# Order dependencies on VectorE in the mixing stage: the inverse's second X before two conv taps and four masked shares, one softmax division before three subtractions of TT

## The chip, the cores and the metric

The kernel runs on one core of one Trainium2 chip. The metric is the device time of one execution in microseconds (us), lower is better. The core has five engines with a queue each: PE (TensorE, matrix products; its weight loads are shown as PEld), DVE (VectorE), ACT (ScalarE), POOL (GpSimd) and SP (SyncE, which issues DMAs here). Each engine takes its instructions strictly in the order in which they were written into its queue, and waits for others by semaphores.

## The reference

Two layers, each a half-step SwiGLU feed-forward, a token mixing and another half-step feed-forward, on 512 tokens of width 1024. Only the mixing is touched. It has three groups of heads side by side:

```python
hn = rms_norm(h, g_mix[l]) * (1.0 + sc2) + sh2
proj = hn @ w_mix_in[l]
p_att, p_rwkv, p_conv = jnp.split(proj, [ATT_PROJ_WIDTH, ATT_PROJ_WIDTH + RWKV_PROJ_WIDTH], axis=-1)
y_att = sliding_window_sink_attention(p_att, ...)   # softmax over a window of 128, blocks of 128 tokens
y_rwkv = rwkv7_time_mix(p_rwkv, ...)                # a linear recurrence over the tokens
y_conv = short_conv_mix(p_conv, conv_w[l])          # u = c_gate * h; three taps over time; b_gate * y
mixed = jnp.concatenate([y_att, y_rwkv, y_conv], axis=-1) @ w_mix_out[l]
h = h + (1.0 + gt2) * mixed
```

## The kernel before, in words

Activations are kept transposed (features on the 128 partitions, 512 tokens along the free dimension). Every large product is made in three passes (`mm3`, L129 to L131), a high and a low part of each operand, and so each block of weights costs a cast to its high part on ACT (L141, `wH`) and a subtraction for its low part on DVE (L143, `wL`), after which its raw buffer is free for the next load from SP (L304).

The mixing (`mix`) weaves four generators into one program: `products()` (the large products `ps_mm`, and the short convolution), `rwkv()`, `attention()` and `inverse()`. A loop with an estimated clock decides whose next step is issued; a scheduler behind it then sets the order on every engine, bounded by data dependencies and by order dependencies written by hand (`tc.add_manual_dep(later, earlier, ORDER)`: the first stands behind the second, and no semaphore is added for it). On PE the small products of the three other generators (all at L787, helper `pe`) stand between the large ones.

The parts that meet around the change, in each layer:

- **The recurrence** is made in chunks of 64 tokens, and needs an inverse of a triangular matrix for each chunk and head, built up in two levels (`invert`, inside `rwkv`). T and TT are the inverse so far and its transpose, each in two tiles (one for each pair of heads). In a level, PE makes `ps_x` (B by T), DVE masks it into X (L1124, six instructions for the two tiles), PE makes `ps_t` from X, and DVE subtracts that from TT, and in the first level from T too (L1135, three instructions for a tile). The second level starts with the other tile first. `ps_x` of the second level goes into the PSUM banks that `ps_t` of the first has left. After the second level PE makes `ps_w` from TT.
- **Attention** goes by four blocks of 128 tokens, with two groups g of heads each. DVE reduces the scores (L1319), ACT makes the exponentials and their sums, DVE adds the sink to the sum (L1356, `den`), inverts it (L1357) and multiplies the 128x512 scores `Sc` by it (L1358: the division, which leaves the shares). PE transposes the shares (`ps_pt`), DVE masks each transpose twice (L1345, `pmc` for the block's own keys, `pmp` for the block before: the masked shares), and PE multiplies them with the values (`ps_av`, four products in the order pmc, pmc, pmp, pmp).
- **The short convolution** makes `conv_u` (L923), its first tap by a scalar (L925), two more taps (L926, L927) and the gate (L929), all on DVE, once for each of two blocks of channels.

In both layers the second level of the inverse falls together with the third block of attention (b == 2) and the first block of channels of the convolution.

Of the kernel before, what the change touches and what calls it, by code (L numbers as in the profile page):

```python
# [12 lines left out]
ALU = mybir.AluOpType  # L13
AXL = mybir.AxisListType
ORDER = mybir.DependencyInfo(mybir.DependencyClass.NoSync, mybir.DependencyReason.DATA)
SYNC = mybir.DependencyInfo(mybir.DependencyClass.Sync, mybir.DependencyReason.DATA)

P = 128
D = 1024
T = 512  # L20
# [6 lines left out]
NB = T // P  # L27
# [43 lines left out]
def trunk_kernel(ctx, tc, ins, out, layers=L, phases=("ffn1", "mix", "ffn2")):  # L71
# [11 lines left out]
    tt, stt, ts = nc.vector.tensor_tensor, nc.vector.scalar_tensor_tensor, nc.vector.tensor_scalar  # L83
# [96 lines left out]
    def cst(name):  # L180
        a, b = CON[name]
        return con[:, a:b]

    def rep(name, n):
        a = cst(name)
        return a.unsqueeze(1).to_broadcast([P, n, a.shape[1]])
# [543 lines left out]
    def mix(l, hn, ss, mp, then, ready):  # L730
# [34 lines left out]
        mu, cwp = prm(l, "mu"), prm(l, "cw")  # L765
        cm = small_.tile([P, KD], F32, name="cm", tag="cg")
        ts(cm, mod[l, 5], 1.0, None, ALU.add)

        done = set()
        k_, r_, v_, yr = {}, {}, {}, {}  # L770
        got = {}

# [50 lines left out]
        def products():  # L823
# [93 lines left out]
            for q in range(2):  # L917
                pt = yield from tile_()
                cc = EA("conv_c")
                nc.scalar.copy(pt.like(cc), pt.view)  # L920
                pt = yield from tile_()
                u = EA("conv_u")
                tt(pt.like(u), pt.view, pt.like(cc), ALU.mult)  # L923
                cv = mp.tile([P, T], F32, name="conv_y", tag="cv", bufs=1) if q == 0 else EA("conv_y")
                ts(cv, u, cwp[:, 4 + q : 5 + q], None, ALU.mult)  # L925
                stt(cv[:, 1:], u[:, : T - 1], cwp[:, 2 + q : 3 + q], cv[:, 1:], ALU.mult, ALU.add)  # L926
                stt(cv[:, 2:], u[:, : T - 2], cwp[:, q : q + 1], cv[:, 2:], ALU.mult, ALU.add)  # L927
                pt = yield from tile_()
                tt(pt.like(cv), pt.view, pt.like(cv), ALU.mult)  # L929
                yc.append(cv)  # L930
# [85 lines left out]
        def rwkv():  # L1016
# [91 lines left out]
            def invert():  # L1108

                T_, TT = got["T"], got["TT"]  # L1110
                X = [S(q, "X", (P, 2, NB, CH)) for q in range(2)]

                def each(q, pts, j, lhs, rhs):
                    for b, e, c in corners:
                        pe(pts[q][e][rows[c ^ e], j, b], lhs[q][rows[c], e, b], rhs[q][rows[c], e, b], start=True, stop=True)

                for lev in range(2):
                    qs = both()
                    pts = quarters("ps_x")
                    for q in qs:  # L1120
                        each(q, pts, 0, LT, T_)
                    for q in qs:
                        for r, e, x in gathered(pts[q], 0):
                            tt(X[q][r, e], x, rep(f"lev{lev}", NB)[r], ALU.mult)  # L1124
                    yield 1.4, 3.2
                    qs = both()
                    pts = quarters("ps_t", 2 - lev)
                    for q in qs:
                        if lev == 0:
                            each(q, pts, 1, TT, X)  # L1130
                        each(q, pts, 0, X, TT)
                    for q in qs:
                        for j, to in ((1, T_), (0, TT))[lev:]:
                            for r, e, x in gathered(pts[q], j):
                                tt(to[q][r, e], to[q][r, e], x, ALU.subtract)  # L1135
                        yield (2.4 - 1.0 * lev if q == qs[0] else 0), 2.8 - 1.2 * lev
            pairs(be, B_, 0, 1)
            LT = [B[:, :, :, 0] for B in B_]
# [9 lines left out]
            qs = both()  # L1148
# [23 lines left out]
            qs = both()  # L1172
# [5 lines left out]
            qs = both()  # L1178
# [9 lines left out]
            qs = both()  # L1188
# [14 lines left out]
            qs = both()  # L1203
# [11 lines left out]
            qs = both()  # L1215
# [15 lines left out]
            qs = both()  # L1231
# [17 lines left out]
            for c in range(1, NC - 1):  # L1249
                qs = both()  # L1250
# [7 lines left out]
            qs = both()  # L1258
# [15 lines left out]
            qs = both()  # L1274
# [13 lines left out]
        def attention():  # L1288

            kt, V, qr, rq = got["kt"], got["V"], got["qr"], got["rq"]  # L1290
            snk = prm(l, "sinks").rearrange("p (i g) -> p g i", g=2)

            def scores(b):
                qs = slice(b * P, (b + 1) * P)
                both = [mp.tile([P, 4, P], F32, name="Sc", tag="Sc", bufs=2) for _ in range(2)]
                if b == 0:
                    for Sc in both:
                        nc.gpsimd.memset(Sc, -1e30)
                for i0 in (0, 2):
                    pts = [psum([P, 2, 2, P], "ps_sc") for _ in range(2)]  # L1300
                    for i in range(2):
                        for g, pt in enumerate(pts):
                            if b:
                                m = pe(pt[:, i].rearrange("p a c -> p (a c)"), qr[rows[g], i0 + i, qs], kt[rows[g], (b - 1) * P : (b + 1) * P], start=True, stop=True)
                            else:
                                m = pe(pt[:, i, 1], qr[rows[g], i0 + i, qs], kt[rows[g], qs], start=True, stop=True)
                            together(m, free[0], SYNC)
                    for Sc, pt in zip(both, pts):
                        if b:
                            nc.scalar.copy(Sc[:, i0 : i0 + 2], pt[:, :, 0])  # L1310
                        free[0] = nc.vector.copy_predicated(Sc[:, i0 : i0 + 2], rep("mq", 2).bitcast(I32), pt[:, :, 1])
                    if i0 == 0:
                        yield 1.06, 1.8
                return both

            def softmax(b, g, Sc):
                rqb = rq.rearrange("p (b i g) -> p b g i", i=4, g=2)[:, b, g]
                mx = small("mx", 4)
                nc.vector.tensor_reduce(mx, Sc, AXL.X, ALU.max)  # L1319
                tt(mx, mx, rqb, ALU.mult)  # L1320
                tt(mx, mx, snk[:, g], ALU.max)
                ts(mx, mx, -1.0, None, ALU.mult)
                es = small("es", 4)
                tt(es, snk[:, g], mx, ALU.add)
                act(es, es, AF.Exp)
                den = small("den", 4)
                for i in range(4):
                    act(Sc[:, i], Sc[:, i], AF.Exp, bias=mx[:, i : i + 1], scale=rqb[:, i : i + 1], accum_out=den[:, i : i + 1])
                return den, es

            made, free = [None], [None]

            def together(m, other, kind=ORDER):

                if other is not None:
                    tc.add_manual_dep(m.ins, other.ins.name, kind, reason="both groups run together")

            def turned(b, Sc):
                pt = psum([P, 4, P], "ps_pt")
                for i in range(4):  # L1340
                    pe(pt[:, i], Sc[:, i], cst("ident"), start=True, stop=True, is_transpose=True)
                both = []
                for name, src in (("mc", b), ("mp", b - 1))[: 1 + (b > 0)]:
                    t = E("p" + name)
                    made[0] = tt(t.rearrange("p (i q) -> p i q", q=P), pt, rep(name, 4), ALU.mult)  # L1345
                    both.append((t, src))
                return both

            for b in range(NB):
                qs = slice(b * P, (b + 1) * P)  # L1350
                pm = []
                both = yield from scores(b)
                dens = [softmax(b, g, Sc) for g, Sc in enumerate(both)]
                for g, (Sc, (den, es)) in enumerate(zip(both, dens)):
                    yield 1.06 * (g == 0), 6.4 if g == 0 else 1.2
                    tt(den, den, es, ALU.add)  # L1356
                    nc.vector.reciprocal(den, den)  # L1357
                    tt(Sc, Sc, den.unsqueeze(2).to_broadcast([P, 4, P]), ALU.mult)  # L1358
                    yield 0, 1.4
                    pm.append(turned(b, Sc))  # L1360
                yield 0.4, 3.0
                po = psum([P, 4, P], "ps_av")
                for n in range(len(pm[0])):
                    for g in range(2):
                        t, src = pm[g][n]
                        m = pe(po[rows[g]].rearrange("p i q -> p (i q)"), V[:, src, rows[g]], t, start=n == 0, stop=n == len(pm[0]) - 1)
                        together(m, made[0])
                free[0] = nc.scalar.copy(qr[:, :, qs], po)
                yield 1.9, 1.0
            done.add("ya")  # L1370
# [29 lines left out]
        for q in range(2):  # L1400
            x = pair("yr")
# [203 lines left out]
    with tc.tile_pool(name="first", bufs=1) as fp:  # L1605
        hn, first, ready, casts = begin(fp)
    for n, (l, p) in enumerate(seq):
# [23 lines left out]
        first = None  # L1631
# [87 lines left out]
```

## Time and profile before

| what | value |
|---|---|
| runs | 1793.84, 1797.02, 1799.68 us; median 1797.02 us |
| the profiled execution's own time | 1795.08 us |
| its span | 1793.3 us (1.8 us of the time lie outside it) |
| PEld | 1613.4 us busy (90%) |
| DVE | 1383.6 us busy (77%) |
| ACT | 856.4 us busy (48%) |
| POOL | 148.3 us busy (8%) |
| mean granted PE clock | 0.999 of full speed |

Busy time says how much of the span an engine spent inside instructions. In the timeline a row is a run of equal instructions: start, length, engine, line, operation, `out<-in`, sizes, count, and in brackets how long the engine had been idle before it and what released it. A list of waits gives, for a waiting engine and tile, who released it: total us, times, longest.

### The profile page before, as it was taken

Reading aid. Unit: us, or ns where it says so; the run is one execution under the profiler, and the core shown is the slowest. Engines: PE = TensorE matmul, PEld = TensorE weight load, DVE = VectorE, ACT = ScalarE, POOL = GpSimd, SP = SyncE. Lnnn points to the kernel's source line nnn. Section 1 sums busy time; section 2 is a strip of 40 time slices with the busy share of each in tenths; the row PEclk is TensorE's granted clock in tenths of the full one; section 3 lists DMA queues with packets and bytes.
Section 4 is the critical chain, followed back from the end, with each engine's and each line's share of the span. In section 5 each row is a group of like instructions: output and inputs, shape, how many; then the busy total and the mean of one; then the engine's idle time right before and its main releaser. Section 6 shows DMA issues by size and latency. Waiting matters only on the chain. (4 is left out here: it accounts for less than half of the span.)

```text
span 1793.3 us, 34028 instructions
## 1 busy us (share of the span) xinstructions
PE 1764.2 (98%) x13952; PEld 1613.4 (90%) x13952; DVE 1383.6 (77%) x2224; ACT 856.4 (48%) x1324; POOL 148.3 (8%) x233
## 2 busy tenths in 40 slices
PE   9999999999999999999999999999999999999998
PEld 7898999987778999899899989999876798999998
DVE  7877678877768877677888777887686788864897
ACT  7452355365444554255355515543644345533563
POOL 0101001000000011100100010010000000010000
PEclk9999999999999999999999999999999999999999
DMA  9667867522133676877737597773320427684764
GB/s 377 222 183 266 225 193 214 184 88 79 51 111 103 178 190 215 266 195 208 238 116 191 170 308 189 205 227 103 119 71 28 142 80 203 183 245 132 202 165 118
DMA packets 95436, 313.08 MB, mean 175 GB/s; under 512 B 10864, under 2 KB 13168, under 8 KB 94256
## 3 DMA queue, kind: packets, MB, share of 16 engines
q1 hardware_dynamic: 65088, 203.68, 33.5%
q0 software_dynamic: 30192, 107.23, 24.2%
q8 instruction: 109, 1.79, 0.4%
q14 instruction: 47, 0.39, 0.1%
HBM read 306.93 MB, written 3.93 MB: 173 GB/s over the span
## 5 line engine op out<-in xcount | busy, mean ns | idle before, releaser
L141 ACT CAST wH<-wraw 128x1024 fp32r<-128x1024 f32 (+2 forms) x276 | 254.2, 928 | 439.9 <-PE ps_mm L130 200.5
L143 DVE TENSOR_TENSOR wL<-wraw,wH 128x1024 fp32r<-128x1024 f32 (+2 forms) x276 | 295.3, 1074 | 111.6 <-ACT wH L141 110.2
L129 PE MATMUL ps_mm<-actH,wH 128*128 128x512 f32 (+1 forms) x700 | 253.9, 363 | 1.5 <-DVE h L343 1.5
L131 PE MATMUL ps_mm<-actH,wL 128*128 128x512 f32 (+1 forms) x700 | 253.4, 362 | 0.1
L130 PE MATMUL ps_mm<-actL,wH 128*128 128x512 f32 (+1 forms) x700 | 253.3, 362 | 0.0
L129 PE MATMUL ps_mm<-hnH,wH 128*128 128x512 f32 (+1 forms) x712 | 248.5, 354 | 3.3 <-ACT hnH L291 3.0
L130 PE MATMUL ps_mm<-hnL,wH 128*128 128x512 f32 (+1 forms) x712 | 246.3, 347 | 0.3
L131 PE MATMUL ps_mm<-hnH,wL 128*128 128x512 f32 (+1 forms) x712 | 245.3, 346 | 0.6 <-DVE wL L143 0.6
L434 PE MATMUL ps_d<-comH,wH 128*128 128x256 f32 x864 | 239.2, 277 | 0.1
L436 PE MATMUL ps_d<-comH,wL 128*128 128x256 f32 x864 | 238.2, 276 | 0.0
L435 PE MATMUL ps_d<-comL,wH 128*128 128x256 f32 x864 | 238.2, 276 | 0.0
L143 DVE TENSOR_TENSOR wL<-sum,wH 128x1024 fp32r<-128x1024 f32 x110 | 134.6, 1225 | 81.3 <-ACT wH L141 81.2
L141 ACT CAST wH<-sum 128x1024 fp32r<-128x1024 f32 x110 | 115.1, 1047 | 122.8 <-PE ps_f L435 39.2
L199 DVE SCALAR_TENSOR_TENSOR wada<-wada,crep 128x1024 f32<-128x1024 f32 x128 | 153.1, 1220 | 26.0 <-DMA wada<-in_wadaT 25.7
L434 PEld LDWEIGHTS ps_d<-comH,wH 128*128 128x128 f32 x864 | 166.2, 192 | 2.0 <-ACT s L460 1.6
L436 PEld LDWEIGHTS ps_d<-comH,wL 128*128 128x128 f32 x864 | 166.3, 192 | 0.0
L435 PEld LDWEIGHTS ps_d<-comL,wH 128*128 128x128 f32 x864 | 166.3, 192 | 0.0
L129 PEld LDWEIGHTS ps_mm<-hnH,wH 128*128 128x128 f32 x712 | 133.9, 190 | 23.6 <-issue 7.6
L129 PEld LDWEIGHTS ps_mm<-actH,wH 128*128 128x128 f32 x700 | 133.1, 190 | 16.8 <-DVE h L343 1.7
L131 PEld LDWEIGHTS ps_mm<-hnH,wL 128*128 128x128 f32 x712 | 135.8, 191 | 13.7 <-DVE wL L143 1.0
L130 PEld LDWEIGHTS ps_mm<-hnL,wH 128*128 128x128 f32 x712 | 135.8, 191 | 13.1 <-DVE hnL L292 1.3
L131 PEld LDWEIGHTS ps_mm<-actH,wL 128*128 128x128 f32 x700 | 133.1, 190 | 15.6 <-DVE wL L143 0.5
(426 smaller groups left out, 4006.0 us busy)
## 6 DMA issues: line engine op xcount, KB each, us to landing
wada<-in_wadaT POOLq DMA_DIRECT2D x126, 512.0 KB, 4.7
wraw<-in_wmi SPq DMA_DIRECT2D x40, 512.0 KB, 3.5
wraw<-in_w2p SPq DMA_DIRECT2D x36, 512.0 KB, 4.2
wraw<-in_w1p SPq DMA_DIRECT2D x32, 512.0 KB, 4.3
wraw<-in_w1o SPq DMA_DIRECT2D x32, 384.0 KB, 4.7
wraw<-in_w2o SPq DMA_DIRECT2D x32, 384.0 KB, 4.1
wraw<-in_w1o SPq DMA_DIRECT2D x32, 320.0 KB, 3.7
sum<-in_w2p SPq DMA_DIRECT2D x18, 512.0 KB, 4.3
```

Of the source, the lines that this page charges most:

```text
L129: mm(acc, wH, xH, start=start, stop=False)
L130: mm(acc, wH, xL, start=False, stop=False)
L131: latest["large"] = mm(acc, wL, xH, start=False, stop=stop)
L141: latest["cast"] = nc.scalar.copy(hi, src)
L143: return nc.vector.tensor_sub(lo, src, hi.bitcast(F32))
L199: stt(w, w, 1.0, crep, ALU.mult, ALU.mult, accum_out=out_)
L434: mm(acc, wH, xH, start=start and i + k == 0, stop=False, skip_group_check=True)
L435: mm(acc, wH, xL, start=False, stop=False, skip_group_check=True)
L436: mm(acc, wL, xH, start=False, stop=k == 3, skip_group_check=True)
```

## The change

Three lists are filled and used for order dependencies; no instruction is added, removed or altered. `held` has the two later taps of the first block of channels and the four masked shares of the third attention block; each must now stand behind the X of the second level. `turns` has the three subtractions of the second TT tile in the first level; each must now stand behind the division of the third block's first group.

```diff
-        done = set()
+        done, held, turns = set(), [], []
...
-                stt(cv[:, 1:], u[:, : T - 1], cwp[:, 2 + q : 3 + q], cv[:, 1:], ALU.mult, ALU.add)
-                stt(cv[:, 2:], u[:, : T - 2], cwp[:, q : q + 1], cv[:, 2:], ALU.mult, ALU.add)
+                held.append(stt(cv[:, 1:], u[:, : T - 1], cwp[:, 2 + q : 3 + q], cv[:, 1:], ALU.mult, ALU.add))
+                held.append(stt(cv[:, 2:], u[:, : T - 2], cwp[:, q : q + 1], cv[:, 2:], ALU.mult, ALU.add))
...
-                            tt(X[q][r, e], x, rep(f"lev{lev}", NB)[r], ALU.mult)
+                            new = tt(X[q][r, e], x, rep(f"lev{lev}", NB)[r], ALU.mult)
+                    for later in held if lev else ():
+                        tc.add_manual_dep(later.ins, new.ins.name, ORDER, reason="the inverse goes first")
...
-                                tt(to[q][r, e], to[q][r, e], x, ALU.subtract)
+                                new = tt(to[q][r, e], to[q][r, e], x, ALU.subtract)
+                                if lev == 0 and j == 0 and q == qs[1]:
+                                    turns.append(new)
...
                     made[0] = tt(t.rearrange("p (i q) -> p i q", q=P), pt, rep(name, 4), ALU.mult)
+                    if b == 2:
+                        held.append(made[0])
...
-                    tt(Sc, Sc, den.unsqueeze(2).to_broadcast([P, 4, P]), ALU.mult)
+                    share = tt(Sc, Sc, den.unsqueeze(2).to_broadcast([P, 4, P]), ALU.mult)
+                    for later in turns if (b, g) == (2, 0) else ():
+                        tc.add_manual_dep(later.ins, share.ins.name, ORDER, reason="shares go first")
```

In the built program the order changes on DVE alone, at these places and in both layers alike. (The changed file has a few lines more, so that its L1137 is L1135 before, L1349 is L1345, and L1362 to L1364 are L1356 to L1358.)

First place, DVE at the end of the inverse's first level, in the first layer: T_4518 and TT_4520 are the second tiles of T and TT. Before:

```order
L1135 TENSOR_TENSOR T_4518<-T_4518,ps_t 128x256
L1135 TENSOR_TENSOR T_4518<-T_4518,ps_t 64x256 x2
L1135 TENSOR_TENSOR TT_4520<-TT_4520,ps_t 128x256
L1135 TENSOR_TENSOR TT_4520<-TT_4520,ps_t 64x256 x2
L1356 TENSOR_TENSOR den<-den,es 128x4 x2
L1357 RECIPROCAL den<-den 128x4 x2
L1358 TENSOR_TENSOR Sc<-Sc,den 128x512 x2
```

and with the change:

```order
L1137 TENSOR_TENSOR T_4518<-T_4518,ps_t 128x256
L1137 TENSOR_TENSOR T_4518<-T_4518,ps_t 64x256 x2
L1362 TENSOR_TENSOR den<-den,es 128x4
L1363 RECIPROCAL den<-den 128x4
L1364 TENSOR_TENSOR Sc<-Sc,den 128x512
L1137 TENSOR_TENSOR TT_4520<-TT_4520,ps_t 128x256
L1137 TENSOR_TENSOR TT_4520<-TT_4520,ps_t 64x256 x2
L1362 TENSOR_TENSOR den<-den,es 128x4
L1363 RECIPROCAL den<-den 128x4
L1364 TENSOR_TENSOR Sc<-Sc,den 128x512
```

The first group's three instructions have moved ahead of the three subtractions, and the two groups, which stood in pairs, now stand apart.

Second place, DVE a little further on, from the low part of a weight block to the gate of the convolution: X_4714 and X_4715 are the two tiles of X. Before:

```order
L143 TENSOR_TENSOR wL<-wraw,wH 128x1024
L926 SCALAR_TENSOR_TENSOR conv_y<-conv_u,par,conv_y 128x511
L1345 TENSOR_TENSOR pmc<-ps_pt,con 128x512
L927 SCALAR_TENSOR_TENSOR conv_y<-conv_u,par,conv_y 128x510
L1345 TENSOR_TENSOR pmp<-ps_pt,con 128x512
L1124 TENSOR_TENSOR X_4715<-ps_x,con 128x256
L1124 TENSOR_TENSOR X_4715<-ps_x,con 64x256 x2
L1124 TENSOR_TENSOR X_4714<-ps_x,con 128x256
L1124 TENSOR_TENSOR X_4714<-ps_x,con 64x256 x2
L1345 TENSOR_TENSOR pmc<-ps_pt,con 128x512
L1345 TENSOR_TENSOR pmp<-ps_pt,con 128x512
L929 TENSOR_TENSOR conv_y<-ps_mm,conv_y 128x512
```

and with the change:

```order
L143 TENSOR_TENSOR wL<-wraw,wH 128x1024
L1124 TENSOR_TENSOR X_4715<-ps_x,con 64x256
L1124 TENSOR_TENSOR X_4715<-ps_x,con 128x256
L1124 TENSOR_TENSOR X_4715<-ps_x,con 64x256
L1124 TENSOR_TENSOR X_4714<-ps_x,con 64x256
L1124 TENSOR_TENSOR X_4714<-ps_x,con 128x256
L1124 TENSOR_TENSOR X_4714<-ps_x,con 64x256
L926 SCALAR_TENSOR_TENSOR conv_y<-conv_u,par,conv_y 128x511
L1349 TENSOR_TENSOR pmc<-ps_pt,con 128x512
L927 SCALAR_TENSOR_TENSOR conv_y<-conv_u,par,conv_y 128x510
L1349 TENSOR_TENSOR pmp<-ps_pt,con 128x512
L1349 TENSOR_TENSOR pmc<-ps_pt,con 128x512
```

The six instructions of X stand directly behind the weight block, and two taps and two masked shares have moved behind them, ahead of the other two masked shares. Behind these rows come, before, the gate (L929), the low part of a 128x768 weight block (L143) and the six subtractions of TT; with the change the gate stands between the subtractions of the two TT tiles, and the weight block behind all six.

Third place, PE, whose order is the same, with the semaphores that its rows wait for, from `ps_t` of the second level to `ps_av` of the third block. Before:

```order
L787 MATMUL ps_t<-TT_4519,X_4714 64x64 [waits DVE_49,PE_49]
L787 MATMUL ps_t<-TT_4519,X_4714 64x64 x15
L787 MATMUL ps_t<-TT_4520,X_4715 64x64 x16
L129 MATMUL ps_mm<-hnH,wH 128x512
L130 MATMUL ps_mm<-hnL,wH 128x512
L131 MATMUL ps_mm<-hnH,wL 128x512
L787 MATMUL ps_av<-pmc,V 64x512
L787 MATMUL ps_av<-pmc,V 64x512 [waits DVE_49]
L787 MATMUL ps_av<-pmp,V 64x512
L787 MATMUL ps_av<-pmp,V 64x512 [waits DVE_49]
```

and with the change:

```order
L787 MATMUL ps_t<-TT_4519,X_4714 64x64 [waits DVE_49,PE_49]
L787 MATMUL ps_t<-TT_4519,X_4714 64x64 x15
L787 MATMUL ps_t<-TT_4520,X_4715 64x64 x16
L129 MATMUL ps_mm<-hnH,wH 128x512
L130 MATMUL ps_mm<-hnL,wH 128x512
L131 MATMUL ps_mm<-hnH,wL 128x512
L787 MATMUL ps_av<-pmc,V 64x512 [waits DVE_49] x2
L787 MATMUL ps_av<-pmp,V 64x512
L787 MATMUL ps_av<-pmp,V 64x512 [waits DVE_49]
```

The first of the four `ps_av` now waits for DVE itself, up to the first group's `pmp`, where an earlier wait of PE had covered it. `ps_t` starts with X_4714, the tile that DVE writes last. In the same way the first and the third product of `ps_x` of the second level now wait for the first and the last subtraction of TT_4520, which free its PSUM banks.

## The prediction

> **What bounds the kernel now.** I read the page's first part, then PE's list of waits, then the timeline of the two places that the change touches.
>
> ```profile
> PE 1764.2 (98%) x13952; PEld 1613.4 (90%) x13952; DVE 1383.6 (77%) x2224; ACT 856.4 (48%) x1324; POOL 148.3 (8%) x233
> ...
> PE ps_t L787 <- DVE X L1124: 4.6, 2, 2.3
> ...
> PE ps_pt L787 <- DVE Sc L1358: 1.7, 2, 0.9
> ```
>
> PE is busy for 98% of the span, so time can be won only where PE stands still, or where its clock is low. Two of its waits belong to the change: `ps_t` for X, 2.3 us in each of the two layers, and `ps_pt` for the division, 0.9 us in each. They add up to 6.3 us. In the first layer they lie here (PE's rows):
>
> ```profile
> 475.85 0.38 PE L131 MATMUL ps_mm<-hnH,wL 128*128 128x512 f32 x1
> 477.09 0.63 PE L787 MATMUL ps_pt<-con,Sc 128*128 128x128 f32 x4 [0.87 <-DVE Sc L1358]
> 477.65 1.16 PE L787 MATMUL ps_x<-T,B 64*64 64x64 f32 x64
> ...
> 484.98 1.16 PE L787 MATMUL ps_t<-TT,X 64*64 64x64 f32 x64 [2.29 <-DVE X L1124]
> ...
> 486.92 1.08 PE L787 MATMUL ps_av<-pmc,V 128*64 128x512 f32 x4
> ...
> 488.78 0.48 PE L129 MATMUL ps_mm<-hnH,wH 128*128 128x512 f32 x1
> ...
> 491.34 1.98 PE L787 MATMUL ps_w<-AX,TT 64*64 64x128 f32 x64
> ```
>
> PE had its work until 476.22 and 482.69, and both times waited for DVE. DVE in the same stretch:
>
> ```profile
> 474.53 1.29 DVE L1135 TENSOR_TENSOR TT<-TT,ps_t 128x256 f32<-128x256 f32 x3
> 475.85 0.24 DVE L1356 TENSOR_TENSOR den<-den,es 128x4 f32<-128x4 f32 x2
> ...
> 476.25 1.29 DVE L1358 TENSOR_TENSOR Sc<-Sc,den 128x512 f32<-128x512 f32 x2
> 477.46 0.68 DVE L923 TENSOR_TENSOR conv_u<-ps_mm,conv_c 128x512 f32<-128x512 f32 x1
> ...
> 478.59 1.22 DVE L143 TENSOR_TENSOR wL<-wraw,wH 128x1024 fp32r<-128x1024 f32 x1
> 479.72 0.74 DVE L926 SCALAR_TENSOR_TENSOR conv_y<-conv_u,par,conv_y 128x511 f32<-128x511 f32 x1
> 480.38 0.68 DVE L1345 TENSOR_TENSOR pmc<-ps_pt,con 128x512 f32<-128x512 f32 x1
> 480.99 0.74 DVE L927 SCALAR_TENSOR_TENSOR conv_y<-conv_u,par,conv_y 128x510 f32<-128x510 f32 x1
> 481.64 0.68 DVE L1345 TENSOR_TENSOR pmp<-ps_pt,con 128x512 f32<-128x512 f32 x1
> 482.24 2.59 DVE L1124 TENSOR_TENSOR X<-ps_x,con 128x256 f32<-128x256 f32 x6
> 484.86 0.69 DVE L1345 TENSOR_TENSOR pmc<-ps_pt,con 128x512 f32<-128x512 f32 x1
> 485.47 0.68 DVE L1345 TENSOR_TENSOR pmp<-ps_pt,con 128x512 f32<-128x512 f32 x1
> 486.07 0.68 DVE L929 TENSOR_TENSOR conv_y<-ps_mm,conv_y 128x512 f32<-128x512 f32 x1
> 486.67 0.95 DVE L143 TENSOR_TENSOR wL<-wraw,wH 128x768 fp32r<-128x768 f32 x1
> 487.53 2.59 DVE L1135 TENSOR_TENSOR TT<-TT,ps_t 128x256 f32<-128x256 f32 x6
> ```
>
> No row has a bracket: DVE does not wait at all from 474.53 to 490.12. It is the bound of this stretch, and PE gets its operands when DVE comes to them. An order can therefore choose which of PE's products is served first; it cannot make DVE's sum smaller. That is the main thing to see here, because all four masked shares are still due before `ps_av`, which stands only 2 us behind `ps_t` on PE.
>
> **The change part by part, first layer.** No duration changes, so I walk DVE and PE through the new order with the distances between starts in the rows above.
>
> The division apart. In pairs, `den`, reciprocal and division of both groups take 477.46 - 475.85 = 1.61. Alone they take, from the fourth block:
>
> ```profile
> 501.13 0.17 DVE L1356 TENSOR_TENSOR den<-den,es 128x4 f32<-128x4 f32 x1 [1.86 <-ACT Sc L1328]
> 501.33 0.18 DVE L1357 RECIPROCAL den<-den 128x4 f32<-128x4 f32 x1
> 501.55 0.69 DVE L1358 TENSOR_TENSOR Sc<-Sc,den 128x512 f32<-128x512 f32 x1
> ```
>
> 0.42 from `den` to the division, since each waits for the one before, and then 0.605 to the next instruction (half of 477.46 - 476.25). Twice 1.03 is 2.05: DVE loses 0.44. The first group's sums are there in time:
>
> ```profile
> 473.20 0.19 ACT L1328 ACTIVATION_READ_ACCUMULATOR Sc<-Sc,mx,rq 128x1 f32 x1
> ```
>
> That is the fourth sum of the group, ended at 473.39; `den` can start at 474.53. The division then runs from 474.95 to 475.64, the three subtractions of TT from 475.56 to 476.85, the second division from 477.30 to 477.99, and `conv_u` starts at 477.90.
>
> `ps_pt` and `ps_x`. From the end of a DVE instruction to PE's start I take 0.15 (X ends at 482.24 + 2.59 = 484.83, `ps_t` starts at 484.98; the division ends at 476.94, `ps_pt` starts at 477.09). The shares are ready at 475.79, before PE needs them at 476.22: the wait of 0.87 is gone. But `ps_x`, 0.56 later, now has a wait that was covered before: its third product needs the bank that the last subtraction of TT frees, at 476.85 + 0.15 = 477.00, where PE would be at 476.81. So 0.19 comes back, and PE is 0.68 ahead.
>
> X and `ps_t`. X stands directly behind the weight block, whose next start is 479.72 + 0.44 = 480.16. Six instructions take 2.62 (482.24 to 484.86) and end at 482.75. PE is there at 482.69 - 0.68 = 482.01 and waits until 482.90. The wait shrinks from 2.29 to 0.89, and PE is 484.98 - 482.90 = 2.08 ahead.
>
> `ps_av`. Behind X now come tap, `pmc`, tap, `pmp` of the first group (0.66, 0.61, 0.65 and 0.60 apart, as in the rows), then `pmc` and `pmp` of the second. They end at 485.38 (first `pmp`), 485.99 and 486.59. PE arrives at 486.92 - 2.08 = 484.84. The first product waits for the first `pmp` until 485.53, which is 0.69; a product takes (488.78 - 486.92) / 4 = 0.465; the second waits for its `pmc` until 486.14; the third and fourth follow, the last `pmp` being ready at 486.74. PE is through at 487.53 where it was at 488.78. **1.25 us are left** of 3.16: three new waits of 0.19, 0.69 and 0.15 and a rest of 0.89 stand where 0.87 and 2.29 were.
>
> What follows. `ps_w` needs TT. The six subtractions, with the gate between them, end at 489.74 and are ready at 489.89; PE comes at 491.34 - 1.25 = 490.09. The slack is 0.2, so the lead passes, just. Behind `ps_w` the rows hang on PE, and nothing there has a time of its own.
>
> The 128x768 weight block ends at 490.70, not 487.62, and that is what lets SP issue the next load:
>
> ```profile
> 487.64 0.33 SPq L304 DMA_DIRECT2D wraw<-in_wmo  x1
> ...
> 506.41 0.83 ACT L141 CAST wH<-wraw 128x768 fp32r<-128x768 f32 x1 [2.10 <-PE ps_mm L130]
> ...
> wraw<-in_wmo SPq DMA_DIRECT2D x16, 384.0 KB, 3.0
> ```
>
> The load would be issued some 3.1 later and land 3.0 later again, near 494; the cast that uses it starts at 506.41 and waits for PE's old weights. I cost this at nothing; it is covered by about 12 us. The gate L929, 1.8 later, feeds a high part cast tens of rows further on: nothing too.
>
> Second layer. The rows are the same to 0.01 until `ps_t`; then the clock differs:
>
> ```profile
> 1370.86 1.16 PE L787 MATMUL ps_t<-TT,X 64*64 64x64 f32 x64 [2.30 <-DVE X L1124]
> ...
> 1371.95 0.68 PE L129 MATMUL ps_mm<-hnH,wH 128*128 128x512 f32 x1
> ...
> 1376.30 0.48 PE L129 MATMUL ps_mm<-hnH,wH 128*128 128x512 f32 x1
> ...
> 1372.00:1374.00 2.00, 2.00 (x8) 0.97 (x7) 1.99 (x5) 0.00 (x0) 0.00 (x0) 0.53 0.04 8
> 1374.00:1376.30 2.30, 2.30 (x8) 0.46 (x4) 1.94 (x5) 0.00 (x0) 0.00 (x0) 0.67 0.55 171
> ```
>
> The granted clock was 0.53 and 0.67 there, and from the first L129 to the next after `ps_av` took 1376.30 - 1371.95 = 4.35, against 488.78 - 486.07 = 2.71 in the first layer. This cold spell costs 1.64. It begins 1.1 behind the wait for X, and I find no other inside the span's body; so I book it to that idle time. With no gap over 0.9 left I take it as gone.
>
> Sum: 2 x 1.25 + 1.64 = **4.1 us**.
>
> [...]
>
> Bounds of what the trace does not show. Best: both waits vanish whole, 3.16 a layer. Worst for the order itself: every `ps_av` behind the last `pmp`, 486.74 + 1.86 = 488.60, still 0.18 ahead in each layer. I take 1.25, because PE's waits are single and go by product.
>
> **Against which time.** The sum is made against the profiled execution, 1795.08 us (span 1793.3): 1790.9. That run lies 1.9 under the median of 1797.02. If the 1.9 is a second spell (1.64, in the first layer), the median would lose 2.5 + 3.3 and come to 1791.2; if it is something else, it loses 4.1 and comes to 1792.9. The mean of the three, 1791.7, is my number.
>
> **The rivals.**
>
> *The waits go whole.* If the masked shares were ready in time (PE's semaphores sit elsewhere than I read them, or DVE overlaps more), 2 x 3.16 + 1.64 = 8.0 us: 1787.1 from the profiled run. For it: the rows of before show no wait of `ps_av`. Against it: DVE has no idle time to give, and the masked shares move 2.6 us later or stay, while PE comes 2 us earlier.
>
> *The spell stays or moves.* The gap of 2.29 in the first layer did nothing, so the spell may hang on something else, such as the small 64x64 products around the wait. Then 2.5 us remain: 1792.6 from the profiled run, 1794.5 from the median.
>
> [...]
>
> That the change does nothing can be ruled out: the built order has moved as it says.
>
> **How the numbers follow.** A measurement of this kernel tells about 0.3% (5.4 us) from no change. Forecast 0.55; since 1791.7 is 5.3 under the median, it falls on either side of that bound alike, and I give it 0.30 faster, 0.25 same. Waits whole 0.15, all faster. Spell stays 0.20, same but for 0.02. Slower mechanism 0.10, of which 0.06 beyond the bound. Together: faster 0.47, same 0.47, slower 0.06. The range 1787 to 1797 holds the forecast, the full gain and the spell that stays, and leaves out most of the slower case.
>
> **What would show it.** Right: no wait of `ps_pt` for the division; a wait of `ps_t` for X near 0.9; new waits of `ps_av` for `pmc` or `pmp` near 0.7; `ps_w` without a wait for TT; no granted clock under 0.97 in the second layer's stretch. Wrong: `ps_av` starting without a wait (the full gain), a wait at `ps_w`, or low clocks in both layers.

## The result, and the profile after

| | before | after |
|---|---|---|
| median | 1799.68 us (11 runs, 1793.84 to 1802.61) | 1793.96 us (11 runs, 1791.88 to 1798.8) |
| ratio after to before | | 0.9978, 95% interval 0.9968 to 0.9989 |
| profiled execution, its span | 1795.08, 1793.3 us | 1794.78, 1793.0 us |

The kernel is faster by 0.22% (0.11% to 0.32%), some 3.9 us. The ratio isn't that of the two medians, which differ by 5.7 us (the means of the runs by 4.7); the text goes by the ratio and its interval. The prediction had 1791.7 us, which lies 5.3 us under the median it started from; its own sum was 4.1. It took 0.3% for the least that a measurement tells from no change, and so gave "same" as much chance as "faster"; with eleven runs on each side the interval is some 0.1% to either side, and a ratio of 1 lies outside it. The two profiled executions differ by 0.3 us only, so the gain isn't read from their spans. It is read from the stretch that the change touches, and from the clocks of all runs.

PE's list of waits, after (three rows of it: who waits, for whom, total us, times, longest):

```profile
PE ps_t L787 <- DVE X L1124: 2.2, 2, 1.1
PE ps_o L787 <- issue: 2.0, 2, 1.1
...
PE ps_av L787 <- DVE pmp L1349: 1.1, 2, 0.5
```

`ps_pt` is gone from the list, the wait for X has halved, and a wait of `ps_av` for a masked share is new. The wait of `ps_o`, of which the prediction had said nothing, had been longer before:

```profile
PE ps_o L787 <- issue: 2.7, 2, 1.5
```

PE's timeline after, first layer, from the last large product ahead of `ps_pt` to the first behind `ps_av`:

```profile
478.21 0.38 PE L131 MATMUL ps_mm<-hnH,wL 128*128 128x512 f32 x1
478.43 0.60 PE L787 MATMUL ps_pt<-con,Sc 128*128 128x128 f32 x4
478.96 1.48 PE L787 MATMUL ps_x<-T,B 64*64 64x64 f32 x64
...
485.41 1.16 PE L787 MATMUL ps_t<-TT,X 64*64 64x64 f32 x64 [1.09 <-DVE X L1124]
...
487.96 1.24 PE L787 MATMUL ps_av<-pmc,V 128*64 128x512 f32 x3 [0.55 <-DVE pmp L1349]
488.87 0.59 PE L787 MATMUL ps_av<-pmp,V 128*64 128x512 f32 x1
489.04 0.59 PE L787 MATMUL ps_av<-pmc,V 128*64 128x512 f32 x1
489.30 1.19 PE L787 MATMUL ps_av<-pmp,V 128*64 128x512 f32 x3
490.42 0.48 PE L129 MATMUL ps_mm<-hnH,wH 128*128 128x512 f32 x1
```

From 478.21 to 490.42 are 12.21 us, where before had 488.78 - 475.85 = 12.93. I call this distance the **stretch**; it does not depend on what happened earlier in the run. In the second layer it is 12.20, where before had 1376.30 - 1361.72 = 14.58 with the cold spell in it. So `ps_av` is passed 0.72 us earlier in a layer, and not 1.25. The four products take 490.42 - 487.96 = 2.46 us; before they took 1.86. DVE, behind which they wait:

```profile
482.66 2.60 DVE L1124 TENSOR_TENSOR X<-ps_x,con 64x256 f32<-64x256 f32 x6
485.29 0.75 DVE L926 SCALAR_TENSOR_TENSOR conv_y<-conv_u,par,conv_y 128x511 f32<-128x511 f32 x1
485.96 0.69 DVE L1349 TENSOR_TENSOR pmc<-ps_pt,con 128x512 f32<-128x512 f32 x1
486.56 0.74 DVE L927 SCALAR_TENSOR_TENSOR conv_y<-conv_u,par,conv_y 128x510 f32<-128x510 f32 x1
487.22 0.69 DVE L1349 TENSOR_TENSOR pmp<-ps_pt,con 128x512 f32<-128x512 f32 x1
487.82 0.68 DVE L1349 TENSOR_TENSOR pmc<-ps_pt,con 128x512 f32<-128x512 f32 x1
488.42 0.68 DVE L1349 TENSOR_TENSOR pmp<-ps_pt,con 128x512 f32<-128x512 f32 x1
```

The first `pmp` ends at 487.91 and the products start at 487.96; the second group's shares end at 488.50 and 489.10, and the last products follow them.

The windows of after, second layer, where before had clocks of 0.53 and 0.67 (start and end, length, busy time of PE, PEld, DVE, ACT, POOL, granted PE clock, DMA share, GB/s), and two windows of the same run near the start of the first layer's mixing:

```profile
1370.00:1372.00 2.00, 1.89 (x67) 1.54 (x67) 2.00 (x4) 0.00 (x0) 0.00 (x0) 1.00 0.04 8
1372.00:1374.00 2.00, 1.46 (x7) 0.65 (x7) 2.00 (x5) 0.00 (x0) 0.00 (x0) 1.00 0.00 0
1374.00:1376.00 2.00, 2.00 (x9) 0.94 (x6) 1.96 (x5) 0.58 (x1) 0.00 (x0) 1.00 0.01 4
```

```profile
352.00:354.00 2.00, 1.96 (x13) 1.77 (x14) 2.00 (x6) 1.47 (x4) 0.00 (x0) 0.88 0.76 292
354.00:356.00 2.00, 2.00 (x11) 2.00 (x11) 2.00 (x6) 1.04 (x3) 0.00 (x0) 0.50 0.06 19
```

The spell of the second layer is gone, and another one stands at a place that the change doesn't touch and that was warm in the trace of before. This is where most of the profiled run's gain went: PE reaches the stretch 2.36 us later than before, some 1.5 of it lost in that spell. Behind the second layer's mixing it is 1.44 us ahead, and between 1743 and 1749 us it loses 1.16 of that again, mostly to waits for DVE in the last feed-forward; the kernel with the division ahead alone, which is late there, loses 0.84 at the same place, so PE's lead isn't the reason, and the cause is open.

### The profile page after: what moved, and what is told of

The parts are those of the page before. It is cut to its first block, busy times and chain, and to the rows that moved or that the text cites. A ratio compares the mean times of both kernels' runs of the same rounds, so it can differ in the third digit from the quotient of the medians.

```text
span 1793.0 us, 34028 instructions
## 1 busy us (share of the span) xinstructions
PE 1767.1 (99%) x13952; PEld 1615.2 (90%) x13952; DVE 1384.7 (77%) x2224; ACT 856.1 (48%) x1324; POOL 148.3 (8%) x233
## 5 line engine op out<-in xcount | busy, mean ns | idle before, releaser
L143 DVE TENSOR_TENSOR wL<-wraw,wH 128x1024 fp32r<-128x1024 f32 (+2 forms) x276 | 295.4, 1075 | 115.1 <-ACT wH L141 114.1
L131 PE MATMUL ps_mm<-actH,wL 128*128 128x512 f32 (+1 forms) x700 | 253.3, 362 | 0.3 <-DVE wL L143 0.3
L131 PE MATMUL ps_mm<-hnH,wL 128*128 128x512 f32 (+1 forms) x712 | 245.7, 347 | 0.6 <-DVE wL L143 0.6
L143 DVE TENSOR_TENSOR wL<-sum,wH 128x1024 fp32r<-128x1024 f32 x110 | 134.6, 1225 | 78.4 <-ACT wH L141 78.1
L131 PEld LDWEIGHTS ps_mm<-hnH,wL 128*128 128x128 f32 x712 | 136.3, 191 | 13.7 <-DVE wL L143 1.0
L130 PEld LDWEIGHTS ps_mm<-actL,wH 128*128 128x128 f32 x700 | 132.9, 190 | 16.0 <-DVE actL L440 0.9
```

Source lines behind the costliest of these rows:

```text
L130: mm(acc, wH, xL, start=False, stop=False)
L131: latest["large"] = mm(acc, wL, xH, start=False, stop=stop)
L143: return nc.vector.tensor_sub(lo, src, hi.bitcast(F32))
```

## The experiments

Two theories stood at first. The first: DVE's order bounds the stretch, so a step gains what it moves on DVE out of the way of the next operand, and costs what it adds to DVE. The second: the two waits are separate, and the gains of the two parts add up. The first four kernels ran on one chip beside 21 runs of the kernel before (median 1796.88 us), the last three on another beside 19 (1797.56 us).

### X ahead alone

```diff
-                    for later in turns if (b, g) == (2, 0) else ():
-                        tc.add_manual_dep(later.ins, share.ins.name, ORDER, reason="shares go first")
```

(against the changed kernel: the divisions stay behind all subtractions.)

> X ahead of the two taps and the four masked shares; the division stays where it was. Measure: the stretch on PE from the last large product ahead of ps_pt (L131) to the first one behind ps_av (L129), first layer: 12.93 us before, 12.21 with the whole change. Theory A (VectorE's order bounds the stretch, and moving the division costs it 0.44 us): X ends at the old 482.31, ps_t does not wait, ps_pt waits 0.87 again, ps_av starts with the first pmp and takes 2.46 instead of 1.86; the stretch is about 11.6, shorter than with the whole change. Theory B (each part takes away its own wait, and the two add): the division's part is missing, so the stretch lies between 12.21 and 12.93.

Median 1792.65 us (11 runs), ratio 0.9976 (0.9967 to 0.9984). PE's timeline:

```profile
477.27 0.38 PE L131 MATMUL ps_mm<-hnH,wL 128*128 128x512 f32 x1
...
478.51 0.63 PE L787 MATMUL ps_pt<-con,Sc 128*128 128x128 f32 x4 [0.87 <-DVE Sc L1364]
...
484.04 1.16 PE L787 MATMUL ps_t<-TT,X 64*64 64x64 f32 x64
...
486.56 1.24 PE L787 MATMUL ps_av<-pmc,V 128*64 128x512 f32 x3 [0.51 <-DVE pmp L1349]
...
489.01 0.48 PE L129 MATMUL ps_mm<-hnH,wH 128*128 128x512 f32 x1
```

The wait for the division is back, and `ps_t` has no wait at all. The stretch is 11.74 us (11.75 in the second layer): 0.46 shorter than with both parts. This is near the first theory's number (11.6); it falls below everything the second allows.

### The division ahead alone

```diff
-                    for later in held if lev else ():
-                        tc.add_manual_dep(later.ins, new.ins.name, ORDER, reason="the inverse goes first")
```

> The first group's division ahead of three subtractions of TT, alone. Theory A: ps_pt no longer waits, but VectorE comes 0.44 us later to X and to the masked shares, and ps_t waits the more; the stretch is 13.37, longer than before by 0.44, and the time is the same or slower by 0.9 us in both layers. Theory B: PE is ahead by the wait that is gone, 0.87 in each layer; the stretch is 12.06.

Median 1799.0 us (11 runs), ratio 1.0009 (1.0000 to 1.0018). PE's timeline, and one window of each layer:

```profile
478.03 0.38 PE L131 MATMUL ps_mm<-hnH,wL 128*128 128x512 f32 x1
478.25 0.60 PE L787 MATMUL ps_pt<-con,Sc 128*128 128x128 f32 x4
...
487.62 1.99 PE L787 MATMUL ps_t<-TT,X 64*64 64x64 f32 x64 [3.49 <-DVE X L1124]
...
494.06 0.48 PE L129 MATMUL ps_mm<-hnH,wH 128*128 128x512 f32 x1
```

```profile
488.00:490.00 2.00, 2.00 (x62) 1.88 (x57) 2.00 (x4) 0.00 (x0) 0.00 (x0) 0.50 0.03 8
```

```profile
1378.00:1380.00 2.00, 2.00 (x22) 1.14 (x15) 1.99 (x5) 0.00 (x0) 0.00 (x0) 0.50 0.03 8
```

`ps_pt` no longer waits, and the wait for X has grown from 2.29 to 3.49 us. From the last L131 to `ps_t` are 9.59 us, 0.46 more than before (484.98 - 475.85 = 9.13): DVE's 0.44 for the two chains that stand apart, and the wait removed is simply waited for later. The stretch is 16.03 us in all, where the first theory had 13.37: the rest is cold. In the first layer two spells follow each other (486.5 to 493.3 us), and the second layer has one (1377.4 to 1380.8). So the second part of the change gains nothing by itself, and inside the change it costs 0.46 us a layer.

### X written twice

```diff
-                    for q in qs:
+                    for q in qs + qs if lev else qs:
                         for r, e, x in gathered(pts[q], 0):
```

(in the kernel before, so that DVE writes X of the second level twice.)

> The kernel before, with X of the second level written twice (the same values), six more instructions of VectorE ahead of ps_t in each layer. The wait of ps_t grows from 2.29 to about 4.9. If the low PE clock follows from PE's idle time, a spell of 3.4 us at half clock stands behind this wait in both layers, and in nearly every run: mean granted clock 0.998, 5.2 us of waits and about 3.3 us of spells, so slower than before by 5 to 7 us (before has some spells itself). If the spells come from something else, their number does not grow (0.999 or 1.000 in most runs) and the time grows by 5.2 us.

Median 1805.16 us (5 runs), ratio 1.0046 (1.0034 to 1.0059). PE's timeline:

```profile
487.48 0.88 PE L787 MATMUL ps_t<-TT,X 64*64 64x64 f32 x32 [3.53 <-DVE X L1124]
488.84 1.13 PE L787 MATMUL ps_t<-TT,X 64*64 64x64 f32 x32 [0.48 <-DVE X L1124]
```

The waits of the first layer are 3.53 and 0.48 and not 4.9 in one piece: the first half of `ps_t` needs only the tile that is finished first, three of the six added instructions ahead of the end. The sign and the spells are as expected: low clocks at `ps_t` in both layers, from 487.8 to 494.7 (two spells in a row) and from 1378.7 to 1382.1. The 8.3 us are more than the 5 to 7 expected: the mean clock of the runs fell to 0.9950 and not to 0.998, so more was lost in spells than one for each layer.

### The inverse ahead of everything that can wait

The whole change, with `conv_u` behind X too, and the three taps, the gate that needs them and two weight low parts behind the fourth block's first masked scores (L1322 in its lines):

```diff
-                tt(pt.like(u), pt.view, pt.like(cc), ALU.mult)
+                made_u = tt(pt.like(u), pt.view, pt.like(cc), ALU.mult)
+                if q == 0:
+                    held.append(made_u)
...
+                if q == 0:
+                    taps.extend(three)
...
+                    if (b, i0) == (3, 0):
+                        latest["inverse"] = free[0]
+                        for later in taps:
+                            tc.add_manual_dep(later.ins, free[0].ins.name, ORDER, reason="the inverse goes first")
...
+        if "inverse" in latest:
+            tc.add_manual_dep(low.ins, latest["inverse"].ins.name, ORDER, reason="the inverse goes first")
```

> The whole change, and conv_u behind X, and all three taps, the gate and the low parts of two weight blocks behind the scores of the fourth block. Theory A: X follows the second division, ps_t and ps_av start without a wait, the four ps_av take 1.86 again; the stretch is about 10.0, nearly 3 us shorter than before in each layer, and the runs about 6 us faster than before from this alone, 0.3 to 0.5%. Rival: the work put off is missed later (a wait of ps_sc, ps_w, ps_gn or of a large product for VectorE or for a weight block), and the lead behind ps_o is no more than the 1.2 us of the change.

Median 1789.72 us (5 runs), ratio 0.9963 (0.9951 to 0.9976), the lowest of all. PE's timeline, and DVE's first row behind the inverse:

```profile
475.73 0.38 PE L131 MATMUL ps_mm<-hnH,wL 128*128 128x512 f32 x1
475.95 0.60 PE L790 MATMUL ps_pt<-con,Sc 128*128 128x128 f32 x4
...
481.76 1.16 PE L790 MATMUL ps_t<-TT,X 64*64 64x64 f32 x64
...
483.69 1.08 PE L790 MATMUL ps_av<-pmc,V 128*64 128x512 f32 x4
...
485.56 0.48 PE L129 MATMUL ps_mm<-hnH,wH 128*128 128x512 f32 x1
```

```profile
488.67 0.45 DVE L1322 COPY_PREDICATED Sc<-con,ps_sc 128x256 f32<-128x256 int32 x1 [2.42 <-ACT Sc L1321]
```

No wait is left on PE inside the stretch, which is 9.83 us in both layers (about 10.0 was expected), and `ps_av` takes 485.56 - 483.69 = 1.87. DVE now stands idle for 2.42 us behind the inverse: here PE is the bound. DVE's sum of work is what it was (1384.7 us busy in both kernels); what pushed PE back was the work with no hurry that stood ahead of X and the shares.

### The taps behind all four masked shares

X ahead alone, with the two taps moved on:

```diff
-                held.append(stt(cv[:, 1:], u[:, : T - 1], cwp[:, 2 + q : 3 + q], cv[:, 1:], ALU.mult, ALU.add))
-                held.append(stt(cv[:, 2:], u[:, : T - 2], cwp[:, q : q + 1], cv[:, 2:], ALU.mult, ALU.add))
+                taps.append(stt(cv[:, 1:], u[:, : T - 1], cwp[:, 2 + q : 3 + q], cv[:, 1:], ALU.mult, ALU.add))
+                taps.append(stt(cv[:, 2:], u[:, : T - 2], cwp[:, q : q + 1], cv[:, 2:], ALU.mult, ALU.add))
...
                     pm.append(turned(b, Sc))
+                    for later in taps if (b, g) == (2, 1) else ():
+                        tc.add_manual_dep(later.ins, made[0].ins.name, ORDER, reason="masked shares go first")
```

> The two held taps are moved on, behind all four masked shares, with the inverse's second X ahead as before and the divisions left together. First theory (the four products of ps_av run as two pairs and take 1.86 us in all once their operands are there; fed one by one by VectorE they took 2.45): ps_av starts without a wait about 2.0 us behind ps_t, takes 1.86 us to the next large product, and the stretch from the last L131 ahead of ps_pt to the first L129 behind ps_av falls from 11.75 to 10.65 us. The compiler's order puts the 128x768 weight block ahead of the subtractions of TT now, which end some 0.9 us later, so that ps_w, which comes 1.1 us earlier, waits about 1.4 us for TT: no gain in the time against the run with X ahead alone, 1792.4 to 1793.5. Rival (a product costs 0.465 us by itself and the waits were set by VectorE alone): ps_av also has no wait and takes 1.86, but with no serial cost in the other run the stretch falls by the wait of 0.51 alone, to 11.2. If ps_w does not wait for TT, the time is 1790.5.

Median 1793.17 us (11 runs), ratio 0.9978 (0.9969 to 0.9987). PE's timeline:

```profile
476.08 0.38 PE L131 MATMUL ps_mm<-hnH,wL 128*128 128x512 f32 x1
...
484.80 1.08 PE L787 MATMUL ps_av<-pmc,V 128*64 128x512 f32 x4
...
486.67 0.48 PE L129 MATMUL ps_mm<-hnH,wH 128*128 128x512 f32 x1
...
490.54 0.67 PE L787 MATMUL ps_w<-AX,TT 64*64 64x128 f32 x16 [1.24 <-DVE TT L1137]
```

`ps_av` has no wait and takes 1.87 us; the stretch is 10.59. So the 0.6 us that `ps_av` lost in the change lay in how it was fed, and not in the products; had each product its own price, the stretch would have fallen to 11.2 only. But the time is no better than with X ahead alone: the 128x768 weight block has come ahead of the subtractions of TT, and `ps_w` now waits 1.24 us for them. The lead is given back one product later.

### The inverse ahead, without the division's part

```diff
-                    for later in turns if (b, g) == (2, 0) else ():
-                        tc.add_manual_dep(later.ins, share.ins.name, ORDER, reason="shares go first")
```

(against the kernel with the inverse ahead of everything that can wait.)

> The kernel in which the inverse goes ahead of conv_u, three taps, the gate and two weight blocks, without the part that puts the third block's division ahead of three subtractions of TT. First theory (that part costs VectorE 0.44 us and so loses where VectorE bounds the stretch, and gains where it doesn't): here VectorE has 2.4 us of idle time behind the stretch, so the division's wait at ps_pt of 0.87 comes back whole, less 0.19 to 0.32 at ps_x; the stretch is 10.5 to 10.6 us against 9.83 with that part, and the time 1790.2 to 1791.2 against 1789.7. Rival (that part is a loss of 0.46 a layer wherever it stands, as between the two kernels of the first comparison): stretch 9.4 and 1788.8.

Median 1791.37 us (9 runs), ratio 0.9973 (0.9963 to 0.9983). PE's timeline:

```profile
476.20 0.38 PE L131 MATMUL ps_mm<-hnH,wL 128*128 128x512 f32 x1
...
477.46 0.63 PE L790 MATMUL ps_pt<-con,Sc 128*128 128x128 f32 x4 [0.88 <-DVE Sc L1375]
...
486.79 0.48 PE L129 MATMUL ps_mm<-hnH,wH 128*128 128x512 f32 x1
```

The stretch is 10.59 us against 9.83. The same part that cost 0.46 us a layer in the change is worth 0.76 a layer where DVE is not the bound. The median is 0.2 over the upper end expected; the two ratios, from two chips, have overlapping intervals, so the difference in time is not shown by itself, and the stretch is.

### The gap filled

```diff
+                    for _ in range(2 * lev):
+                        for q in qs:
+                            each(q, pts, 0, TT, TT)
                     for q in qs:
                         if lev == 0:
                             each(q, pts, 1, TT, X)
```

> The kernel before, with the products of TT by TT written twice into ps_t's bank ahead of the inverse's second product, which overwrites them: 2.2 us of 64x64 products in the 2.29 us in which TensorE waits for X. Nothing else moves; the real products start at 484.9 to 485.2 as before. First theory (the cold spells at this place come from TensorE's idle time): no clock under 0.97 within 12 us behind ps_t in either layer, mean clock of the runs 0.999 instead of 0.998, and the time 2.0 us under the kernel before, ratio 0.9985 to 0.9992. Rival (the spells come at random or from the small products): clock 0.998 and ratio 1.000 to 1.0005.

Median 1803.07 us (5 runs), ratio 1.0035 (1.0022 to 1.0047). PE's timeline:

```profile
482.68 0.38 PE L131 MATMUL ps_mm<-hnH,wL 128*128 128x512 f32 x1
484.41 0.33 PE L787 MATMUL ps_t<-TT 64*64 64x64 f32 x4 [1.35 <-DVE X L1124]
485.29 2.02 PE L787 MATMUL ps_t<-TT 64*64 64x64 f32 x122 [0.56 <-DVE X L1124]
...
489.05 0.80 PE L787 MATMUL ps_t<-TT,X 64*64 64x64 f32 x35 [1.28 <-issue]
```

This failed as an experiment. The filling products wait for X themselves: `ps_t` of the second level takes the banks out of which X reads `ps_x`, so they are free only when X has been made. The gap was not filled but cut in three, and the products meant to fill it ran behind X. It does not test the rival that it was made for; a filler in banks of its own wasn't tried. It does show one thing: in the second layer a spell (1378.1 to 1381.5) stands in the row of `ps_t`, where the longest single wait was 1.35 us.

### The clocks of all runs

Every run lists its span and its mean granted clock. A spell of half clock over 3.41 us (1372.11 to 1375.52 in the profiled run of before) takes about 0.001 off the mean, so span times (1 - clock) is what a run lost in spells, to within the clock's third decimal; the means over runs are finer. The rest is span times clock. (The kernel with the cut gap is left out.)

The chip of the change's own runs is not on record, nor are the clocks of the eleven runs of before beside them; the mean time of those eleven, 1798.8 us, is 1.7 above that of the 40 runs in the first row. So the first two rows are compared with care; the kernels of the other rows are compared with before on their own chip (mean rest 1791.4 beside the first four kernels, 1791.6 beside the others).

| kernel | runs | mean clock | mean rest, us | longest wait of `ps_t` | layers of its profiled run with a spell behind `ps_t` |
|---|---|---|---|---|---|
| before (both chips) | 40 | 0.9979 | 1791.5 | 2.30 | 1 of 2 |
| the change | 11 | 0.9991 | 1790.7 | 1.09 | 0 of 2 |
| X ahead alone | 11 | 0.9991 | 1789.0 | none | 0 of 2 |
| taps behind the shares | 11 | 0.9991 | 1790.0 | none | 0 of 2 |
| inverse ahead, no division's part | 9 | 0.9991 | 1788.4 | none | 0 of 2 |
| inverse ahead of everything | 5 | 0.9984 | 1785.1 | none | 0 of 2 |
| division ahead alone | 11 | 0.9973 | 1792.1 | 3.49 | 2 of 2 |
| X written twice | 5 | 0.9950 | 1793.9 | 3.53 | 2 of 2 |

With a wait of about 3.5 us a spell came 4 times of 4, with 2.3 us once in 2, with 1.1 or none 0 times of 10. The mean clock says the same of the runs that were not profiled: 0.0012 of 1793 us, or some 2.2 us, are lost less where the wait is 1.1 or gone (the fastest kernel apart). For X ahead alone against before, on one chip, the means of the times differ by 1796.94 - 1792.39 = 4.55 us: 2.4 in the rest, which is twice 12.93 - 11.75 = 1.18, and 2.1 in spells. The 0.9984 of the fastest kernel comes from five runs only; its profiled run has a spell at 510.7 to 514.1 us, directly behind the row of `ps_o`, in which PE stood idle for 1.9 us.

The traces also show a difference between the two layers of before. By their records of the clock a spell lasts 3.41 us (before: 1372.11 to 1375.52) or twice that. The two waits of `ps_t` ended at 484.98 and at 1370.86 us. For each layer, the window that begins 1.25 us behind that end (with the columns of the windows above):

```profile
486.23:489.64 3.41, 3.41 (x15) 1.59 (x16) 3.36 (x7) 0.58 (x1) 0.00 (x0) 1.00 0.30 75
1372.11:1375.52 3.41, 3.41 (x9) 1.32 (x11) 3.36 (x7) 0.00 (x0) 0.00 (x0) 0.50 0.32 91
```

In the first layer the clock stayed full behind a wait of 2.29 us, in the second it was half behind one of 2.30. So the same wait brought a spell in one layer only; what decides that isn't shown.

## Why the prediction was right or wrong

Two steps of it failed: the price of `ps_av` (2.46 us where 2.00 were booked, so that 0.72 us of the lead were left in a layer and not 1.25), and the step from the profiled run to the median (a second spell that the change would remove; the clocks show fewer). What bounds the stretch was right.

**Right: what bounds the stretch.** DVE does, and the two waits did not add up; `ps_pt` lost its wait, X kept one, `ps_av` got one. The rival that the waits go whole falls by the rows (12.21 us where it would have been 12.93 - 3.16 = 9.77; the kernel with the inverse ahead of everything that can wait came to 9.83), and so does the slower case (a chance of 0.10), as no spell stands in the change's two stretches (that a wait cut in pieces can still bring one, the kernel with the cut gap shows).

**Right in size, not followed to its end: the division's part.** The 0.44 us that DVE loses with the chains apart measured 0.47 (12.21 against 11.74) and 0.46 (9.59 against 9.13). The prediction booked the wait of `ps_pt` as gone and carried the 0.44 along DVE, but did not add the two up: with DVE as the bound, that part alone is a loss, and the change without it has a stretch 0.46 shorter.

**`ps_x` and `ps_t`, nearly.** `ps_x` lasts 1.48 us instead of 1.16, a re-wait of 0.32 and not 0.19; the wait for X is 1.09 and not 0.89; the lead at `ps_t` is 9.13 - 7.20 = 1.93 and not 2.08.

**Wrong: the price of `ps_av`.** The prediction gave each of the four products 0.465 us, one after another, let the second wait for its own `pmc`, and had them through 2.00 us behind their start. They took 2.46. The single records of before start two by two (486.92, 486.92, 487.40, 487.40): the products of the two groups run together, and 1.86 us is the time of two pairs. (Each product has two records, so these four are the first pair.) When the second group's shares come 0.6 us behind the first's, the first product runs without its partner. Of the error of 0.53 us a layer (1.25 against 0.72) 0.46 lies here. With all shares ready, in two other kernels, the four took 1.87.

**Not foreseen: `ps_o`.** The idle time inside this row fell from 1.53 to 1.10 us in the first layer, and PE's lead grew behind it:

```profile
512.20 0.27 PE L787 MATMUL ps_o<-B,AX 64*64 64x64 f32 x1 [1.53 <-issue]
513.40 0.27 PE L787 MATMUL ps_o<-B,AX 64*64 64x64 f32 x2 [1.10 <-issue]
```

(Before, then after.) Against the trace of before PE is 2.36 us late ahead of the first layer's stretch and 1.20 behind `ps_o`, then 1.20 late and 1.44 early in the second layer: 1.16 and 2.64 (with the spell), 3.8 in all. So the sum of 4.1 came out near what the two layers gained by luck, by errors of opposite sign: 0.53 us too much for the stretch in each layer, and 0.43 and 0.25 for `ps_o` left out. The profile names no releaser for this hole. In each of the nine traces it stands in this row, once in each layer, 0.80 to 1.91 us long, whatever PE's lead. In the traces of before and after it ends 1.28 to 1.41 us behind the end of a 16 KB transfer on a queue that the profile calls "instruction" (first layer, before: transfer from 509.90 to 510.84, hole to 512.20; after: 510.77 to 511.99, and 513.40). That PE waits there for its next instructions is a guess from these times, and not shown.

**Wrong: the step to the median.** This moved the number from 4.1 to 5.3 us. The prediction took the 1.9 us between the profiled run and the median for a second spell, which the change would remove too. The 1.9 hung on three runs; with eleven the median is 1799.68, and 4.6 above the profiled run. Spells were the right cause of much of the spread (over the 40 runs of before, span and clock have a correlation of -0.74), but not all of them belong to this place. Before, the 40 runs lose 3.8 us to low clocks on the mean, and the change's runs 1.6, which stay (of the 2.4 us in the profiled run of before, 0.7 lie in its last 1.3 us). That is 2.2 us less, between the one spell and the two that the prediction priced (1.64 and 3.3), but the runs compared may be of different chips. With 2.16 us of idle time (1.16, and 2.64 less the spell's 1.64) this gives 4.4; measured were 3.9, with an interval of 2.0 to 5.8. The 5.3 lies inside that interval too, so it is the clocks that speak against the step, and not the time.

**The spell that stays or moves.** This rival was half right: the spell at `ps_t` went in every kernel whose wait there fell to 1.1 us or less, and spells elsewhere go on, so that a single profiled run can lose at another place what it gained. That the wait alone brings a spell is not shown either: before, the clock stayed 1.00 behind a wait of 2.29 us and was 0.50 behind one of 2.30.

**What follows behind.** `ps_w` has no wait for TT after the change, as forecast with a slack of 0.2; the slack is real, for the kernel with the taps last pushed the subtractions back and waited 1.24 us there. The weight block moved by 3.1 us cost nothing that the waits show.

## What to carry to other kernels

Where one engine works without a break and another waits for it, move the work that nobody waits for behind the whole group of operands, as far as the next idle time, and follow the chain to the product after the next: taps that went past the shares only brought a weight block ahead of the next operand. An order that removes a wait but adds work to the engine in front can be a loss while that engine is the bound and a gain as soon as it isn't, so such parts are tried again after each other one. Before a level is explained by a spell, split each run into its span times clock and the rest, and use the mean of many runs, for one profiled run holds whichever spells it happened to meet.

## What the runs showed of the hardware

- A wait of 3.5 us of PE inside a busy stretch came with a spell of half clock in all four cases seen, one of 2.3 us in one of two. In two of the four, two spells followed each other (486.5 to 493.3 and 487.8 to 494.7 us, clock 0.50); in the first of them PE took 6.44 us from `ps_t` to the large product behind `ps_av`, where before it took 3.80.
- Spells lasted 3.41 us (before: 1372.11 to 1375.52, clock 0.50) or twice that (the division ahead alone: 486.5 to 493.3). Before, a wait of 2.30 us in the second layer brought one, and a wait of 2.29 us in the first layer did not (clock 1.00 from 486.23 to 489.64).
- Two products of `ps_av` that write different halves of its partitions ran at the same time: by the records of before they started in pairs (486.92 twice, 487.40 twice); four took 1.87 us when fed together and 2.46 when their operands came 0.6 us apart.
- Long rows of 64x64 products show holes with no releaser: 0.80 to 1.91 us in `ps_o` (1.53 before and 1.10 after, in the first layer), and 1.28 in the doubled row of `ps_t`. In `ps_o`, before and after, they end 1.28 to 1.41 us behind the end of a 16 KB transfer on the queue "instruction"; what PE waits for there isn't shown.
